# A trunk layer whose attention opens in a written-out order: keys first, two queries inside the first steps, modulation pairs behind both heads' transposes

## The chip, the cores and the metric

The kernel runs on one core of a Trainium2 chip. The metric is device time in microseconds (us), the median of three runs; a profiled execution is one further run whose trace is read here. PE is TensorE, DVE VectorE, ACT ScalarE, POOL GpSimd, SP the engine that issues most transfers.

## The reference, cut to what matters

One layer works on 128 context tokens and 512 latent tokens of width 1024. Six modulation vectors (shift, scale and gate, twice) come from the conditioning by a matrix `w_ada` of 1024 x 6144. The attention has 16 query heads in 4 groups with one key head each, of width 64. Behind it come a short convolution, gates, an output matrix and a feed-forward part.

```python
def mixer(u, p, rope_tabs, ctx_k, ctx_v):
    z = u @ p["w_in"]
    q, k, v, b_gate, c_gate, x_in, g_att, g_conv = jnp.split(z, idx, axis=-1)
    q = rms_norm(q.reshape(B, N, N_HEADS, HEAD_DIM), p["q_norm"])
    k = rms_norm(k.reshape(B, N, N_KV_HEADS, HEAD_DIM), p["k_norm"])
    ...
        q_used = apply_axial_rope(q, rope_tabs)
        keys = jnp.concatenate([ctx_k, apply_axial_rope(k, rope_tabs)], axis=1)
        vals = jnp.concatenate([ctx_v, v], axis=1)
    att = block_attention(q_used, keys, vals) @ p["w_att_out"]
    conv = (b_gate * dwconv3(c_gate * x_in, p["conv_w"])) @ p["w_conv_out"]
    merged = jax.nn.sigmoid(g_att) * att + jax.nn.sigmoid(g_conv) * conv
    return merged @ p["w_o"], k, v

def trunk_layer(h, ada, p, rope_tabs, ctx_k, ctx_v):
    sh1, sc1, g1, sh2, sc2, g2 = jnp.split(ada, N_ADA, axis=-1)
    u = rms_norm(h, p["g_pre1"]) * (1 + sc1) + sh1
    mo, k, v = mixer(u, p, rope_tabs, ctx_k, ctx_v)
    h = h + g1 * rms_norm(mo, p["g_post1"])
    ...
```

Context tokens attend to context tokens only and carry no rotary position.

## The kernel before

The 640 tokens are five tiles of 128: tile 0 is the context, tiles 1 to 4 are latent, and a sixth key tile holds the cached keys. Every matrix product is taken three times (`mm3`, L163): both operands are split into a rounded high part and the rest, and the products high-high, high-low and low-high are summed (L164 to L166). A weight block of 128 x 1024 arrives by one transfer of 512 KB into one of three `raw` buffers. Weights that belong to `w_in` or `w_att_out` are units: `cut_hi` (L585) or `split` writes the high part on ACT and the low part, `wlo`, on DVE. The modulation blocks are used as they are. PSUM gives three double banks (`ps2`, tag s2) and two single ones (`ps1`, tag s1).

**Prologue.** Norm, first modulation, and the key and value products of all tiles (`kvp`). A scheduler orders the instructions of this part by a model of their times, and its reach goes on through the opening of the attention, to L576. From L578 on (`manual_schedule`) PE, ACT and DVE keep the order of the text. POOL and SP are ordered by the scheduler everywhere.

**Opening of the attention.** `k_post` (L543) treats one key tile: it copies the values (L544), rotates the keys (`rotate`, L434, on DVE, the last addition at L446 on DVE for keys and on POOL for queries), takes squares on ACT (L450), their sums on DVE (L456) and the factor on POOL (`factors`, L453: a scaling at L457 and a power at L458), and doubles the scaled keys side by side with four ACT instructions (L556). `k_turn` (L374, its transposes by `turn` at L371) transposes a tile on PE, copies it on ACT (L378, `KH` or `KCH`) and takes its low part on DVE (L379). `q_mm` (L482) computes a query tile of the first group with 24 matmuls (`q_part`, L472, two units of four rows each), rotates it (`q_rotate`) and takes its factor. `q_turn` (L488) transposes it at L491, and writes `QH` on ACT and `QL` on DVE (L497). The loop over t runs keys two tiles ahead of queries (`K_AHEAD`), and with queries 2 and 4 goes one modulation pair each (`EARLY`).

**Steps.** For each group g of four there are nine steps: step 0 for the context, steps 1 to 8 for two halves of the queries, two pairs of heads and two tiles. `Step` (L597) computes the scores of two heads (L505), `most` their maximum on DVE (L625), `exps` the exponential on ACT (L640), `shares` the division on POOL (L650); `turned` transposes the shares of the step before on PE (L663) and copies them (L668), and `values` (L670) multiplies them with the values. In between lie, in the text's order: query tiles 0 to 2 of the next group in steps 3, 5 and 7, and 3 and 4 in steps 0 and 2; in group 3 instead three parts of a gate (`gate_part`, L695, unit 16, kept in the raw buffer `held[0]`, L525); units 10 to 17 for the next group and the gates; and the modulation pairs. A pair (`ada_use`, L535) is two blocks, 16 matmuls each at L216, into one single bank; `ada2_keep` adds the bank to `acc` on DVE. After group 3 the second gate (`gate1_part`, L788, unit 17) is computed around the last transposes, and `cut_upto(19)` (L150) cuts units 18 and 19.

**Loads.** The order of the loads behind unit 9 is a list, `ring` (L513), of modulation blocks ("a"), units ("u") and the buffer held ("g"). `ring_used(n)` says that n entries have been read and issues loads up to three entries further on. A load goes to the buffer that the pool gives out next, and SP issues it when the buffer's last reader is done.

## Time and profile before

| | before |
|---|---|
| median of 3 runs | 1165.39 us (1165.21 to 1167.93) |
| profiled execution | 1163.74 us |
| its span in the trace | 1161.9 us |
| mean granted clock of PE | 0.987 |
| instructions in the span | 19659 |
| moved by DMA | 129.58 MB |

The span is the time from the first to the last instruction of the trace; 1.84 us of the execution lie around it. The busy share of an engine is its busy time over the span; the strip of granted clocks has 40 slices of 29 us, in tenths of full speed. A timeline row has its start, its duration, the engine, the line, the operation, output and inputs, how many equal instructions follow one another, and in brackets the idle time before it with the instruction that ended it. The attention of this kernel runs from about 68 to 297 us of the span.

### The profile page before, as it was taken

The numbers are of one execution on the slowest core, as the hardware profiler recorded it, in microseconds if no ns is written. First come the engines' busy times: TensorE is split into PE (matmuls) and PEld (weight loads), VectorE is DVE, ScalarE is ACT, GpSimd is POOL, SyncE is SP. The second block draws the span as 40 slices with busy tenths as digits, with TensorE's granted clock in tenths as the row PEclk, the third lists the DMA queues.
The fourth block names the chain that finished last, engine by engine and source line by source line (L and its number), as shares of the span: only waits on it lengthen the run. The fifth ranks groups of instructions, "written<-read, shape, count | busy, mean of one in ns | idle before, by whom it ended". The sixth has DMA issues, their size and how long they took to land. (4 is left out here: it accounts for less than half of the span.)

```text
span 1161.9 us, 19659 instructions
## 1 busy us (share of the span) xinstructions
PE 1128.8 (97%) x7949; PEld 1030.3 (89%) x7949; DVE 791.1 (68%) x1267; ACT 572.0 (49%) x987; POOL 147.4 (13%) x193
## 2 busy tenths in 40 slices
PE   7997999999999999999999999999999999999997
PEld 5785788888899999999999988999999999998785
DVE  4475666655555788988745446888877788778634
ACT  4255566665433544554542246555454555545432
POOL 1034555564000000000000012000000000000001
PEclk7997999999999999999999999999999999999999
DMA  8925231322222323323232543333332333314732
GB/s 268 264 59 172 86 111 61 110 74 74 88 72 60 91 74 92 91 73 100 83 109 74 201 144 124 95 114 114 102 100 91 95 114 102 113 60 165 245 103 90
DMA packets 181400, 129.58 MB, mean 112 GB/s; under 512 B 6274, under 2 KB 163518, under 8 KB 181310
## 3 DMA queue, kind: packets, MB, share of 16 engines
q1 hardware_dynamic: 180526, 128.04, 35.8%
q8 instruction: 62, 1.02, 0.3%
q10 hardware_dynamic: 784, 0.30, 0.1%
q14 instruction: 28, 0.23, 0.1%
HBM read 116.87 MB, written 11.45 MB: 110 GB/s over the span
## 5 line engine op out<-in xcount | busy, mean ns | idle before, releaser
L844 PE MATMUL b<-ZB,whi 128*128 128x322 f32 x1024 | 229.5, 311 | 1.7 <-DVE C L855 1.7
L844 PEld LDWEIGHTS b<-ZB,whi 128*128 128x128 f32 x1024 | 173.4, 189 | 5.5 <-DVE C L855 3.9
L844 PE MATMUL b<-ZB,wlo 128*128 128x322 f32 x512 | 159.4, 311 | 0.0
L844 PE MATMUL b<-MT,whi 128*128 128x320 f32 x608 | 134.1, 308 | 0.0
L844 PEld LDWEIGHTS b<-MT,whi 128*128 128x128 f32 x608 | 101.6, 188 | 0.0
L844 PEld LDWEIGHTS b<-ZB,wlo 128*128 128x128 f32 x512 | 96.2, 188 | 0.0
L844 PE MATMUL b<-MT,wlo 128*128 128x320 f32 x304 | 93.8, 308 | 0.0
L650 POOL TENSOR_TENSOR pr<-pr,sm 128x640 f32<-128x640 f32 x64 | 79.5, 1253 | 80.6 <-DVE sm L649 74.7
L831 ACT ACTIVATE whi<-SUM 128x1024 fp32r<-128x1024 f32 x40 | 42.2, 1055 | 81.7 <-DVE SUM L1298 79.2
L1328 DVE SCALAR_TENSOR_TENSOR Y<-C,cffn,Y 128x642 f32<-128x642 f32 x88 | 77.7, 885 | 1.8 <-ACT Y L1323 0.2
L139 DVE TENSOR_TENSOR wlo<-raw,whi 128x1024 fp32r<-128x1024 f32 (+1 forms) x33 | 36.1, 1094 | 59.9 <-ACT whi L138 59.5
L640 ACT ACTIVATE pr<-s,mx,rq 128x640 f32<-128x640 f32 x64 | 56.6, 885 | 36.4 <-DVE mx L627 36.0
L844 PE MATMUL b<-UH,whi 128*128 128x320 f32 x228 | 70.5, 309 | 0.0
L844 PE MATMUL b<-UL,whi 128*128 128x320 f32 x228 | 70.4, 309 | 0.0
L625 DVE TENSOR_REDUCE mx<-s 128x1 f32<-128x640 f32 x64 | 52.5, 820 | 26.2 <-PE s L505 26.1
L844 PE MATMUL b<-UH,wlo 128*128 128x320 f32 x228 | 70.2, 308 | 0.0
L835 DVE TENSOR_TENSOR wlo<-raw,whi 128x1024 fp32r<-128x1024 f32 (+1 forms) x51 | 50.4, 1020 | 25.0 <-ACT whi L831 24.1
L164 PE MATMUL s<-whi,UH 128*128 128x256 f32 (+1 forms) x200 | 65.5, 327 | 1.9 <-ACT UH L351 1.1
L831 ACT ACTIVATE whi<-WB 128x1024 fp32r<-128x1024 f32 x38 | 40.1, 1056 | 54.9 <-DVE WB L939 54.9
L852 ACT ACTIVATE p<-b 128x322 f32<-128x322 f32 (+1 forms) x78 | 34.2, 439 | 62.1 <-PE b L844 62.1
L165 PE MATMUL s<-wlo,UH 128*128 128x256 f32 (+1 forms) x200 | 61.8, 309 | 0.0
L166 PE MATMUL s<-whi,UL 128*128 128x256 f32 (+1 forms) x200 | 59.8, 311 | 0.0
(305 smaller groups left out, 2940.3 us busy)
## 6 DMA issues: line engine op xcount, KB each, us to landing
raw<-in_w_in_dram SPq DMA_DIRECT2D x48, 512.0 KB, 3.7
RAW<-in_w_up_dram SPq DMA_DIRECT2D x40, 512.0 KB, 4.0
raw<-in_w_ada_dram SPq DMA_DIRECT2D x32, 512.0 KB, 4.0
raw<-in_w_down_dram SPq DMA_DIRECT2D x22, 512.0 KB, 4.4
araw<-in_w_ada_dram SPq DMA_DIRECT2D x16, 512.0 KB, 7.4
actd<-Y SPq DMA_DIRECT2D x18, 321.0 KB, 2.5
AFB<-actd SPq DMA_DIRECT2D x18, 321.0 KB, 5.5
raw<-in_w_conv_out_dram SPq DMA_DIRECT2D x9, 512.0 KB, 3.3
```

What stands on the lines that cost most here:

```text
L139: V.tensor_tensor(out=lo[:, :n], in0=raw, in1=hi[:, :n].bitcast(F32), op=ALU.subtract)
L164: PE.matmul(out, ah, bh, start=start, stop=False)
L165: PE.matmul(out, ah, bl, start=False, stop=False)
L166: PE.matmul(out, al, bh, start=False, stop=stop)
L625: V.tensor_reduce(out=mx, in_=self.sc[h], axis=AX.X, op=ALU.max, negate=True)
L640: S.activation(pr, self.sc[h], AF.Exp, bias=mx, scale=rs, accum_out=sm)
L650: G.tensor_tensor(out=pr, in0=pr, in1=sm.broadcast_to((128, NTOK)), op=ALU.mult)
L831: S.activation(to[0], raw, AF.Copy)
L835: V.tensor_tensor(out=lo, in0=raw, in1=hi.bitcast(F32), op=ALU.subtract)
L844: PE.matmul(out, p[:, ws], q[:, k, :], start=start and k == 0 and n == 0, stop=stop and k == 3 and n == 2, skip_group_check=True)
L852: S.activation(t, pair[j][b], AF.Copy)
L1328: V.scalar_tensor_tensor(out=y, in0=crows(j)[i][:, d:d + NACT], scalar=cffn[:, 44 * d + o:44 * d + o + 1], in1=y, op0=ALU.mult, op1=ALU.add)
```

## The change

The order of the opening is written out by hand. `manual_schedule` is entered ahead of the attention's pool, so that PE, ACT and DVE follow the text from there on. `k_post`, `rotated`, `q_mm` and `turn` are replaced by smaller functions (`k_rotate`, `k_copies`, `k_factors`, `k_double`, `k_done`, `q_first`, `q_rotate_first`, `q_factors`), which are called in one list: keys first, in the order of tiles 0, 2, 4, 1, 3, with query tiles 0 to 2 of the first group between them. Two key tiles share a double bank for their transposes. The keys' last rotary addition goes to POOL. Key tile 3 is transposed at the start of step 0, and queries 3 and 4 of the first group are computed in steps 0 and 1. First queries use single banks only. An exponential of one element is placed ahead of the keys, and a sigmoid of one element behind the last step's first transposes.

No modulation pair is in the opening any more; each group has four, in steps 2, 4, 6, 8 of group 0 and steps 1, 4, 6, 8 of the others, behind the transposes of both heads instead of between them, and its addition follows at once. The list of loads has a new order, with units 10 and 11 first. The low cuts of units 11, 13 and 15 are taken in two halves, the second in the next step. Unit 17 is cut in step 6 of group 3 instead of step 8, and `cut_upto(19)` comes ahead of most of the second gate.

```diff
@@ -36,15 +36,11 @@
 OFF = 192
 BLKS = ((0, 320), (320, 640))
 ZB = 4
-Q2 = 2
-K_AHEAD = 2
-KADD = 1
 F_LOAD = 5
 F_TAB = 6
 XB = 4
 WARM = 20
 ROWS_AT = 2
-EARLY = (2, 4)
 SEGS = ((0, NCTX), (NCTX, NTOK))
...
         KCL = kvp_.tile([128, NKV, 128], F32R, name="KCL")
         VV = kvp_.tile([128, 6, 256], F32, name="VV")
-        def turn(x, idn):
-            p = ps1()
+        def k_turn(t, kd, p):
             for h in range(4):
-                PE.transpose(p[:, h * 128:(h + 1) * 128].bitcast(x.dtype), x[:, h].rearrange("p s d -> p (s d)"), idn)
-            return p.rearrange("p (h c) -> p h c", c=128)
-        def k_turn(t, kd):
-            p = turn(kd, ident)
+                PE.transpose(p[:, h * 128:(h + 1) * 128], kd[:, h].rearrange("p s d -> p (s d)"), ident)
+        def k_done(t, p):
+            p = p.rearrange("p (h c) -> p h c", c=128)
             c0 = 0 if t in (0, 5) else t * 128
             kh, kl = (KCH, KCL) if t == 0 else (KH[:, :, c0:c0 + 128], KL[:, :, c0:c0 + 128])
...
+    fixed = ctx.enter_context(ExitStack())
+    fixed.enter_context(tc.manual_schedule(engines={mybir.EngineType.PE, mybir.EngineType.Activation, mybir.EngineType.DVE}))
...
-            (V if i == 1 and KADD else G).tensor_tensor(out=out, in0=out, in1=tm, op=ALU.add)
+            G.tensor_tensor(out=out, in0=out, in1=tm, op=ALU.add)
...
-        def q_mm(g, t):
-            pz = (ps2() if t >= Q2 else ps1())[:, 0:256]
-            q_part(pz, g, t, range(KT))
-            q_rotate(pz, g, t)
-            factors(squares(pz), rq[g][:, t, :])
...
-        ring = [("a", i) for i in range(6)] + [("u", 10), ("u", 11)] + [("a", i) for i in range(6, 14)] + [("u", 12)]
-        ring += [("a", i) for i in (14, 15)] + [("u", 13)] + [("a", i) for i in range(16, 20)] + [("u", 14)]
-        ring += [("a", i) for i in (20, 21)] + [("u", 15)] + [("a", i) for i in range(22, 26)]
-        ring += [("a", i) for i in (26, 27)] + [("u", 16), ("g", 0)] + [("a", i) for i in range(28, 32)] + [("u", 17)]
+        def ada_raws(a, b):
+            return [("a", i) for i in range(2 * a, 2 * b)]
+        ring = [("u", 10), ("u", 11)] + ada_raws(0, 4) + [("u", 12)] + ada_raws(4, 5) + [("u", 13)] + ada_raws(5, 8) + [("u", 14)]
+        ring += ada_raws(8, 9) + [("u", 15)] + ada_raws(9, 12) + ada_raws(12, 13) + [("u", 16), ("g", 0)] + ada_raws(13, 14)
+        ring += [("u", 17)] + ada_raws(14, 16)
...
-        ring_load(2)
-        kds = {}
-        def k_post(t):
-            S.activation(VV[:, 5 if t == 0 else t, :], kvp[t][:, 256:512], AF.Copy)
-            if t < 3:
+        ring_load(3)
+        warm = at.tile([128, 1], F32, name="warm", bufs=1)
+        S.activation(warm, mhalf[:, 0:1], AF.Exp)
+        kds, kfs, rks, sqs, pzs = {}, {}, {}, {}, {}
+        def k_rotate(t):
+            if t in (0, 2):
+                room = wide([128, 2, NKV, HD], "room")
+                kf, tm = room[:, 0], room[:, 1]
+                kds[t] = wide([128, NKV, 2, HD], "room")
+            else:
                 room = at.tile([128, 5, 256], F32, tag="PT", name=nm("room"), bufs=3)
                 kf, tm = (room[:, i, :].rearrange("p (h d) -> p h d", d=HD) for i in range(2))
-                kd = room[:, 2:4, :].rearrange("p a (b s d) -> p (a b) s d", s=2, d=HD)
-            else:
-                room = wide([128, 2, NKV, HD], "room")
-                kf, tm = room[:, 0], room[:, 1]
-                kd = wide([128, NKV, 2, HD], "room")
-            rk = at.tile([128, 4], F32, tag="rk", name=nm("rk"), bufs=NT)
-            rotated(kvp[t][:, 0:256], t, 1, kf, tm, rk)
+                kds[t] = room[:, 2:4, :].rearrange("p a (b s d) -> p (a b) s d", s=2, d=HD)
+            kfs[t] = kf
+            rks[t] = at.tile([128, 4], F32, tag="rk", name=nm("rk"), bufs=NT)
+            rotate(kvp[t][:, 0:256], t, 1, kf, tm)
+        def k_copies(t):
+            sqs[t] = squares(kvp[t][:, 0:256])
+            S.activation(VV[:, 5 if t == 0 else t, :], kvp[t][:, 256:512], AF.Copy)
+        def k_factors(t):
+            factors(sqs.pop(t), rks[t])
+        def k_double(t):
             for h in range(NKV):
-                S.activation(kd[:, h], kf[:, h:h + 1, :].broadcast_to((128, 2, HD)), AF.Copy, scale=rk[:, h:h + 1])
+                S.activation(kds[t][:, h], kfs[t][:, h:h + 1, :].broadcast_to((128, 2, HD)), AF.Copy, scale=rks[t][:, h:h + 1])
             if t == 0:
                 nc.scalar.dma_start(new_v.rearrange("t h d -> t (h d)"), VV[:, 5, :])
-                nc.scalar.dma_start(new_k, kd[:, :, 0, :])
-            kds[t] = kd
-        for t in range(NT + K_AHEAD):
-            if t < NT:
-                k_post(t)
-            i = t - K_AHEAD
-            if i < 0:
-                continue
-            q_mm(0, i)
-            if i in EARLY:
-                ada_use(EARLY.index(i))()
-            k_turn(i, kds[i])
-            if i > 0:
-                q_turn(0, i - 1)()
-        q_turn(0, NT - 1)()
-        fixed = ctx.enter_context(ExitStack())
-        fixed.enter_context(tc.manual_schedule(engines={mybir.EngineType.PE, mybir.EngineType.Activation, mybir.EngineType.DVE}))
+                nc.scalar.dma_start(new_k, kds[t][:, :, 0, :])
+        def q_first(t):
+            pzs[t] = ps1()[:, 0:256]
+            q_part(pzs[t], 0, t, range(KT))
+        def q_rotate_first(t):
+            q_rotate(pzs[t], 0, t)
+            sqs["q", t] = squares(pzs[t])
+        def q_factors(t):
+            factors(sqs.pop(("q", t)), rq[0][:, t, :])
+        q_first(0)
+        k_rotate(0)
+        k_copies(0)
+        k_rotate(2)
+        k_factors(0)
+        k_copies(2)
+        k_rotate(4)
+        k_factors(2)
+        k_copies(4)
+        k_rotate(1)
+        k_factors(4)
+        k_double(0)
+        k_copies(1)
+        q_first(1)
+        k_rotate(3)
+        k_factors(1)
+        k_double(2)
+        k_copies(3)
+        q_rotate_first(0)
+        k_factors(3)
+        q_factors(0)
+        p02 = ps2()
+        k_turn(0, kds[0], p02[:, 0:512])
+        k_turn(2, kds[2], p02[:, 512:1024])
+        k_double(4)
+        k_done(0, p02[:, 0:512])
+        k_done(2, p02[:, 512:1024])
+        q_first(2)
+        q_rotate_first(1)
+        q_factors(1)
+        low = q_turn(0, 0)
+        low()
+        k_double(1)
+        p41 = ps2()
+        k_turn(4, kds[4], p41[:, 0:512])
+        k_turn(1, kds[1], p41[:, 512:1024])
+        k_done(4, p41[:, 0:512])
+        k_double(3)
+        k_done(1, p41[:, 512:1024])
+        low = q_turn(0, 1)
+        low()
+        q_rotate_first(2)
+        q_factors(2)
...
-            def low():
-                V.tensor_tensor(out=lo, in0=raw, in1=hi.bitcast(F32), op=ALU.subtract)
-                ring_used(1)
+            def low(a=0, b=1024):
+                V.tensor_tensor(out=lo[:, a:b], in0=raw[:, a:b], in1=hi[:, a:b].bitcast(F32), op=ALU.subtract)
+                if b == 1024:
+                    ring_used(1)
...
-        n_ada, last, after1, after2 = len(EARLY), None, [], []
+        n_ada, last, halves = 0, None, []
+        after1, after2 = [], []
         for g in range(NKV):
             if g + 1 < NKV:
                 q_begin(g + 1)
             for i in range(9):
                 low1, low2, late_hi = [], [], []
                 st = Step(g) if i == 0 else Step(g, ((i - 1) // 4, (i - 1) // 2 % 2, (i - 1) % 2))
-                turn = {0: (g, 2) if g else None, 2: (g, 3) if g else None, 4: (g, 4) if g else None}.get(i)
-                if g + 1 < NKV and i in (5, 7):
-                    turn = (g + 1, (i - 5) // 2)
-                if turn and i != 2:
-                    low1.append(q_turn(*turn))
+                first = {0: (g, 2) if g else None, 5: (g, 4)}.get(i)
+                then = {0: None if g else (0, 2), 2: (g, 3), 5: (g + 1, 0), 7: (g + 1, 1)}.get(i)
+                if then and then[0] == NKV:
+                    then = None
+                if g == 0 and i == 0:
+                    p = ps1()
+                    k_turn(3, kds[3], p)
+                    k_done(3, p)
+                if first:
+                    low1.append(q_turn(*first))
                 if i == 2:
                     hi, lo = values(g)
                     hi()
...
                 for h in range(1 if st.ctx else 2):
                     st.most(h)
                     st.exps(h)
-                for f in low1:
+                for f in low1 + halves:
                     f()
+                halves = []
                 qt = None
                 if g + 1 < NKV and i in (3, 5, 7):
                     qt = (g + 1, (i - 3) // 2)
-                elif g and i in (0, 2):
-                    qt = (g, 3 + i // 2)
+                elif i == 0 or i == (2 if g else 1):
+                    qt = (g, 3 if i == 0 else 4)
                 blk = (i - 3) // 2 if g + 1 == NKV and i in (3, 5, 7) else None
                 if i in (4, 6, 8) or (i == 1 and g):
                     hi, lo = values(*((g - 1, 3) if i == 1 else (g, (i - 4) // 2)))
...
                     q_part(pz, *qt, range(4, KT))
                 if blk is not None:
                     gate_part(pz, c0, c1, range(4, KT))
-                if i in ((0, 2, 4, 6, 8) if g == 0 else (1, 4, 6)):
-                    low2.append(ada_use(n_ada))
-                    n_ada += 1
-                if turn and i == 2:
-                    low2.append(q_turn(*turn))
                 if not st.ctx:
                     st.shares(1)
-                u = {1: 10 + 2 * g, 2: 11 + 2 * g}.get(i) if g + 1 < NKV else {2: 16, 8: 17}.get(i)
+                u = {1: 10 + 2 * g, 2: 11 + 2 * g}.get(i) if g + 1 < NKV else {2: 16, 6: 17}.get(i)
                 if u:
-                    low2.append(cut_hi(u))
+                    low = cut_hi(u)
+                    if i == 2 and g + 1 < NKV:
+                        low2.append(lambda low=low: low(0, 512))
+                        halves = [lambda low=low: low(512, 1024)]
+                    else:
+                        low2.append(low)
+                if then and then != (0, 2):
+                    low2.append(q_turn(*then))
                 for f in low2:
                     f()
                 for f in after2:
...
                 if last and not last.ctx:
                     last.turned(1)()
                 after1, after2 = [], []
+                if i in (4, 6, 8) or i == (1 if g else 2):
+                    ada_use(n_ada)()
+                    n_ada += 1
                 if qt:
                     def rotation(pz=pz, qt=qt):
                         q_rotate(pz, *qt)
...
                         rotation()
                 if blk is not None:
                     S.activation(held[0][:, c0:c1], pz, AF.Copy)
+                if then == (0, 2):
+                    low = q_turn(0, 2)
+                    low()
                 last = st
         assert 2 * n_ada == 4 * KT and at_ring[0] == len(ring)
         state["limit"], state["next"] = 1 << 20, 18
...
         gate1_part(0, range(4))
         ada2_fold(acc)
         last.turned(0)(True)
+        S.activation(warm, mhalf[:, 0:1], AF.Sigmoid)
+        cut_upto(19)
         gate1_part(0, range(4, KT))
         last.turned(1)()
         gate1_part(1, range(4))
         hi, lo = values(NKV - 1, 3)
         hi()
         lo()
-        cut_upto(19)
         gate1_part(1, range(4, KT))
     atts.close()
```

More of the change, by code (lines that the diff above doesn't have):

```diff
@@ L417, in trunk_layer @@
             if f == F_TAB:
-                k_turn(5, ck)
+                p = ps1()
+                k_turn(5, ck, p)
+                k_done(5, p)
                 ptr = ps1()
@@ L458, in factors @@
             G.tensor_tensor(out=rstd, in0=ssq, in1=mhalf[:, :4], op=ALU.pow)
-        def rotated(pz, t, i, out, tm, rstd):
-            rotate(pz, t, i, out, tm)
-            factors(squares(pz), rstd)
         QH, QL, rq, qfs = {}, {}, {}, {}
@@ L705, in trunk_layer @@
                 st = Step(g) if i == 0 else Step(g, ((i - 1) // 4, (i - 1) // 2 % 2, (i - 1) % 2))
[L706 to L710 removed]
+                first = {0: (g, 2) if g else None, 5: (g, 4)}.get(i)
[3 more added lines that the diff above has]
+                if g == 0 and i == 0:
+                    p = ps1()
+                    k_turn(3, kds[3], p)
+                    k_done(3, p)
+                if first:
+                    low1.append(q_turn(*first))
                 if i == 2:
```

## The prediction

> **What bounds the kernel now.** I read the page first: the busy shares and the strip of granted clocks.
>
> ```profile
> PE 1128.8 (97%) x7949; PEld 1030.3 (89%) x7949; DVE 791.1 (68%) x1267; ACT 572.0 (49%) x987; POOL 147.4 (13%) x193
> PEclk7997999999999999999999999999999999999999
> ```
>
> TensorE is the bound. What can be won is its idle time, and busy time that passes at a lowered clock: the fourth slice of the strip (87 to 116 us) is such a place, and it is where the rewritten order ends. So I cut that stretch, and the attention stage behind it, into windows (the columns are busy us and instructions of PE, PEld, DVE, ACT and POOL, then the clock, the DMA share and GB/s).
>
> ```profile
> 68.00:88.00 20.00, 18.77 (x177) 17.33 (x175) 13.62 (x42) 12.95 (x39) 11.19 (x19) 1.00 0.24 66
> 88.00:92.00 4.00, 1.49 (x34) 1.01 (x34) 2.55 (x8) 3.97 (x13) 2.49 (x4) 1.00 0.46 136
> 92.00:96.00 4.00, 2.07 (x20) 1.52 (x24) 2.08 (x6) 1.57 (x5) 2.32 (x4) 0.75 0.78 247
> 96.00:100.00 4.00, 4.00 (x44) 3.07 (x32) 1.37 (x3) 0.00 (x0) 0.00 (x0) 0.50 0.60 172
> 100.00:104.00 4.00, 2.57 (x14) 1.85 (x12) 1.73 (x7) 3.31 (x6) 2.38 (x2) 0.50 0.32 96
> 104.00:108.00 4.00, 3.60 (x32) 2.24 (x29) 3.86 (x8) 2.17 (x5) 0.44 (x2) 0.54 0.39 111
> 108.00:112.00 4.00, 3.02 (x38) 2.46 (x39) 2.42 (x5) 1.82 (x4) 2.11 (x2) 1.00 0.73 213
> 112.00:297.00 185.00, 180.70 (x1870) 148.56 (x1869) 113.48 (x306) 117.24 (x252) 104.02 (x105) 1.00 0.29 85
> ```
>
> Of the 24 us from 88 to 112, PE is idle for 24 - (1.49+2.07+4.00+2.57+3.60+3.02) = 7.25 us. The clock is at half for 2 + 4 + 4 + 3.7 = 13.7 us, with about 10.9 us of busy PE in it, of which half, 5.4 us, would not be needed at full clock. From 112 to 297 the idle time is 185 - 180.7 = 4.3 us in all, so there nearly everything is PE's own work and moved work keeps its price. PE's own timeline gives the single waits (in brackets, with what ended them) and the prices of its groups:
>
> ```profile
> 80.91 0.36 PE L164 MATMUL s<-whi,UH 128*128 128x256 f32 x1
> ...
> 83.94 1.08 PE L216 MATMUL s<-raw,s 128*32 128x128 f32 x32
> ...
> 106.51 1.08 PE L216 MATMUL s<-raw,s 128*32 128x128 f32 x16
> 108.98 0.54 PE L216 MATMUL s<-raw,s 128*32 128x128 f32 x12 [1.39 <-DMA raw<-in_w_ada_dram]
> ...
> 110.25 0.41 PE L505 MATMUL s<-KH,QH 64*128 64x320 f32 x2
> ...
> 166.44 0.41 PE L505 MATMUL s<-KH,QH 64*128 64x320 f32 x1 [0.59 <-ACT PT L668]
> ...
> 294.24 0.42 PE L164 MATMUL s<-UH,whi 128*128 128x320 f32 x1 [0.80 <-ACT whi L589]
> ...
> 296.29 0.41 PE L166 MATMUL s<-UH,wlo 128*128 128x320 f32 x1 [1.50 <-DVE wlo L592]
> ```
>
> The last two are the end of the stage: unit 17 is cut in step 8, too late for gate 1, and PE stands for 2.3 us. The row at 108.98 is the pattern that matters below: a modulation pair whose block is loaded only when another buffer has just come free.
>
> **Part 1, the opening (68 to 112 us).** The same matmuls run; what differs is their order and what each waits for. A first query is 24 matmuls (80.91 to 83.94: 3.0 us). Keys are now prepared all together, and their chain runs over POOL, whose order is not written by hand. Its prices, and those of the other engines:
>
> ```profile
> L458 POOL TENSOR_TENSOR rk<-ssq,mhalf 128x4 f32<-128x4 f32 x5 | 5.1, 1012 | 0.3
> ...
> L446 POOL TENSOR_TENSOR qf<-qf,zt 128x256 f32<-128x256 f32 x4 | 2.9, 732 | 3.4 <-DVE qf L445 3.3
> L457 POOL TENSOR_SCALAR ssq<-ssq 128x4 f32<-128x4 f32 x10 | 2.0, 203 | 62.2 <-DMA raw<-in_w_ada_dram 58.1 <-DVE ssq L456 3.6
> ```
> ```profile
> 69.59 0.42 DVE L456 TENSOR_REDUCE ssq<-sq 128x4 f32<-128x256 f32 x1 [0.79 <-ACT sq L450]
> 69.92 0.48 DVE L443 TENSOR_TENSOR room<-s,tabk 128x128 f32<-128x128 f32 x2
> 70.32 0.41 DVE L445 TENSOR_TENSOR room<-s,tabk 128x256 f32<-128x256 f32 x1
> ...
> 71.71 0.41 DVE L446 TENSOR_TENSOR room<-room 128x256 f32<-128x256 f32 x1
> ```
> ```profile
> 103.72 1.45 DVE L592 TENSOR_TENSOR wlo<-raw,whi 128x1024 fp32r<-128x1024 f32 x1 [1.27 <-ACT whi L589]
> ```
> ```profile
> 73.97 1.28 ACT L556 ACTIVATE room<-room,rk 128x128 f32<-128x128 f32 x4 [0.31 <-POOL rk L458]
> ...
> 88.60 1.28 ACT L634 ACT_TABLE_LOAD   x1
> ```
>
> The four key additions go from VectorE (0.41 each, the row at 71.71) to POOL (0.73 each): 2.9 us more on POOL, ahead of the factors (0.20 + 1.01 per tile). In the changed program POOL does an addition, a factor pair (1.21), an addition, 0.20, an addition, 0.20 and the power (1.01) before tile 2's factor: 0.73+1.21+0.73+0.20+0.73+0.20+1.01 = 4.8 us. It can begin when the first rotated tile leaves VectorE: at 70.73 in before, behind a reduction that waited 0.79 for squares; the changed order puts the rotation ahead of that, so near 69.8. It ends near 74.6; ScalarE then doubles tile 2 (a quarter of 1.28 per head). PE, two queries (3.0 each) from where before has its first, is through them and tile 0's transposes near 73.8 by my estimate. So its first wait is about 1.5 us.
>
> By the same hand chain (prices above, 0.4 per copy or square, order from the program) I get eight more. The largest two: the first query's transposes wait for the bank of query 1, which is free once it is rotated and squared. Its rotation stands on VectorE behind the low parts of key tiles 0 and 2, each behind ScalarE's copy: from 78.0, 0.6 + 0.7 + 0.6 + 0.7 (half the 1.45 that a cut of 1024 columns takes in the row at 103.72), some 0.9 of rotation and 0.4 of square end at 81.9, and PE is done with query 2 at 79.8: 2.1. And the transposes of query tile 3 in step 2 wait for the bank of query 4, whose rotation stands behind the low cut of unit 10 (1.45) and the turned context shares: 2.3. The rest: query 2 for the squares of query 0, 0.7; key tile 1 for its copy, 0.4; key tile 3 for the bank that the low part of query tile 1 frees, 1.5; query 3 for squares, 0.65; query 4 in step 1 for squares behind the context exponentials, 1.5; the transposes of step 2 for the exponentials of step 1, 1.3. The exponential's table load (1.28 at 88.60) moves ahead of the keys, where ScalarE waits for PE: 0. Together 1.5 + 2.1 + 2.3 + 0.7 + 0.4 + 1.5 + 0.65 + 1.5 + 1.3 = 12 us, strewn over 73 to 107 us. So many in 34 us should again bring down the clock; I put two stretches of 3.4 us at half, 1.7 us lost in each, against four before. That makes 12 + 3.4 = 15.4 us lost. Before lost 7.25 + 5.4 in 88 to 112 and 20 - 18.77 = 1.23 in 68 to 88: 13.9. **Opening: +1.5 us.** Bounds: half my waits and one slow stretch give 6 + 1.7 - 13.9 = -6.2; all of them with four slow stretches 18.8 - 13.9 = +4.9.
>
> With two early modulation pairs, one pair of step 0 and one query's transposes gone from it, step 3 should begin its scores near 110.25 - 3.5 + 1.5 = 108 (104 to 110). That is no gain: the pairs cost 1.0 each (32 matmuls, 83.94 to 84.95) wherever they stand, and from 112 on PE has 98% of its time full. The later loop runs 4 pairs in every group instead of 5, 3, 3, 3 plus two, the same 16.
>
> **Part 2, steps of the later groups.** A pair's sum now frees its bank later: the fourth query of step 2 in groups 1 and 2 waits for that addition behind other VectorE work, about 0.9 to 1.3 by the prices above, where the scores there wait 0.59 now (the row at 166.44): +0.3 each, **+0.6**, bounds 0 and 1.4. A short wait at gate 16 in group 3 changes its cause and not its size: 0. The halved cut of units 11, 13 and 15 lets the maximum of the next step in between; VectorE is busy 113 of 185 us there: 0, bounds -0.3 and +0.3.
>
> **Part 3, one self-made wait.** In the changed order of loads the raw buffers, of which one is held from group 3 on, come out such that the 30th modulation block goes into the buffer of the 29th. Both belong to one pair, the one of step 6 of group 3, now behind both heads' transposes: its load can be issued only when PE has read the first half, and PE's next instruction is the second half. Nothing covers it. The price is a lone load, 512 KB. In before the same kind of load waits for a low cut, that of the row at 103.72. From its end at 105.17 to PE's restart at 108.98 are 3.81 us, of which only 1.39 showed there, since other matmuls lay in between. Here none do: **+3.8**. Bounds: 2.4, the 3.81 less one 1.4 that may pass in PE's last matmul and the restart, and 4.4, that much the slower from a load beside others.
>
> **Part 4, the clock after it.** Not shown alone in before: a bare gap of 3.8 us. Nearest rows are the first lowering of the run and its neighbours:
>
> ```profile
> 5.30:8.70 3.40, 1.64 (x13) 1.22 (x12) 1.51 (x2) 2.84 (x7) 1.91 (x5) 1.00 1.03 415
> 8.70:12.10 3.40, 3.38 (x16) 3.27 (x16) 2.73 (x6) 2.62 (x7) 2.82 (x6) 0.50 1.15 315
> 12.10:15.50 3.40, 3.40 (x54) 2.53 (x56) 2.74 (x7) 1.58 (x3) 0.06 (x1) 1.00 1.21 290
> ```
>
> A stretch of 3.4 us with 1.64 busy is followed by one at half, and a full one ends it: 1.7 us lost. The opening shows the dear end: four stretches, 6.8 lost. A gap of 3.8 spans one stretch or parts of two, and PE's work after it is dense (98%), so I take one stretch, 1.7, and in one case of three a second: **+2.3**, bounds 0 and 6.8.
>
> The Trainium skill has a rule here ("TensorE: Matmul & The Clock Gate", Part 1): the clock is judged in free-running windows of some 3.4 us, a wholly idle one halves it and a busy one restores it. The rows at 5.30 and 8.70 agree in the length, but there the clock fell behind a stretch that was half busy. By the page alone a gap of 3.8 us holds a whole window in 0.4 of 3.4 cases, and this term would be 0.2, the sum 2.1 lower.
>
> **Part 5, the end.** Unit 17 is cut in step 6, so 0.80 + 1.50 = **-2.3** goes; what is late next is unit 18, whose load waits for the last pair in step 8 but whose reader comes a whole gate 1 later: 0. The final cuts, made earlier, take small waits on low parts: **-0.4**, bounds -0.8 and 0.
>
> **Sum.** The profiled execution took 1163.74 us (span 1161.9 and 1.84 around it), 1.65 below the median of 1165.39. 1163.74 + 1.5 + 0.6 + 3.8 + 2.3 - 2.3 - 0.4 = **1169.2**, which is 3.8 over the median of the runs. A measurement of this kernel can tell about 0.3%, 3.5 us, from no change: slower begins at 1168.9, faster below 1161.9. The forecast stands just over the limit, with 1167 to 1172 as its own range (opening +0.5 to +3, load 3.0 to 4.4).
>
> **Rivals.** *The opening goes through* (0.14): place, 73 to 107 us; half the waits vanish because ScalarE and POOL run further ahead than my chain has them, and one stretch is slow. Price -6.2, and one slow stretch behind the load: 1163.74 - 6.2 + 0.6 + 3.8 + 1.7 - 2.7 = 1160.9. It decides if step 3's scores begin before 103. For it: 13.9 us are there to be won. Against: POOL's chain alone outlasts what PE has to do meanwhile.
>
> *The clock holds behind the load wait* (0.25): the gap lies across two stretches, both busy enough, and the strip stays at 1.00: 1169.2 - 2.3 = 1166.9, or 1165.2 with one slow stretch less in the opening too; I take 1166. For it: PE is dense on both sides of the gap. Against: the rows at 5.30 and 8.70, where a stretch busy by half was enough. The skill's page named above sides with this rival.
>
> *The clock stays down behind the load wait* (0.13): the opening's 13.7 us at half repeat, 6.8 lost in place of 2.3: 1173.7. For it: nothing but the opening's rows; against: the opening had waits all through it.
>
> *The load isn't late* (0.03): the block lands in another buffer, the change doesn't do what I read from it, and parts 3 and 4 go: 1163.1.
>
> **Numbers.** The forecast has 0.45, four fifths of it over 1168.9. Slower: 0.36 + 0.13 = 0.49. Same: its lowest fifth 0.09, the clock that holds 0.25, the load not late 0.03: 0.37. Faster: 0.14. The range from 1163 to 1173 leaves out the first rival and about half of the third, 0.2 in all.
>
> **What would show it.** In the changed profile: a wait of PE of 3.4 to 4.4 us for DMA at the modulation matmul in the last third of group 3 (near 275 to 285 us), a clock of 0.5 behind it; no wait for `wlo` at gate 1; step 3's scores at 104 to 110; fewer slow stretches between 84 and 112; key doubling as the first releaser of PE near 75. I am wrong if the scores of step 3 start after 111, if no DMA wait is seen in group 3, or if the clock there stays 1.00 and the time still grows.

## The result, and the profile after

The changed kernel takes 1170.15 us (median of 9 runs, 1167.21 to 1171.18), the kernel before in the same comparison 1166.09 (9 runs, 1164.19 to 1167.93). The ratio is 1.0033, 95% interval 1.0022 to 1.0043: slower by 3.9 us. Forecast were 1169.2, or 3.8 over the median of before.

The profiled execution took 1170.93 us, span 1169.1. Against the profile of before that is 7.2 us more, but 1163.74 lies below before's nine runs, so the two profiles show the places and the medians the size.

Page of the changed kernel, busy shares and granted clock:

```profile
PE 1131.1 (97%) x7949; PEld 1034.7 (89%) x7949; DVE 791.9 (68%) x1266; ACT 573.0 (49%) x989; POOL 150.3 (13%) x197
PEclk8997999999899999999999999999999999999999
```

The work of PE is the same to 2.3 us. Windows of the changed kernel (columns as in the prediction):

```profile
68.00:88.00 20.00, 15.45 (x101) 12.98 (x99) 9.63 (x28) 12.41 (x38) 11.96 (x19) 0.91 0.14 39
88.00:112.00 24.00, 19.37 (x146) 16.23 (x146) 15.35 (x37) 11.55 (x28) 11.36 (x14) 0.72 0.14 40
112.00:284.00 172.00, 168.68 (x1822) 141.16 (x1824) 108.68 (x294) 110.94 (x239) 98.48 (x101) 1.00 0.34 100
284.00:288.10 4.10, 0.45 (x20) 0.18 (x13) 2.51 (x4) 1.24 (x2) 1.28 (x2) 1.00 0.48 142
288.10:304.00 15.90, 15.90 (x137) 13.23 (x137) 5.75 (x15) 6.52 (x14) 4.22 (x4) 0.68 0.22 63
```

In the opening the idle time has moved forward: 4.55 us in 68 to 88 (1.23 before) and 4.63 in 88 to 112 (7.25 before), 9.2 in all against 8.5. Then comes one hole, 284 to 288.1, and behind it 15.9 us without a gap at a mean clock of 0.68. The waits of the opening and the hole on PE's timeline (the row of SP is the load's issue, from SP's own timeline):

```profile
76.72 1.21 PE L367 MATMUL s<-ident,room 128*128 128x128 f32 x4 [1.96 <-ACT room L561]
78.40 0.58 PE L160 MATMUL s<-whi,UH 128*128 128x256 f32 x1 [0.48 <-ACT sq L450]
...
83.32 0.44 PE L481 MATMUL s<-ident,qf 128*128 128x128 f32 x2 [0.55 <-ACT sq L450]
...
84.52 1.20 PE L367 MATMUL s<-ident,room 128*128 128x128 f32 x4 [0.33 <-ACT room L561]
...
89.11 1.12 PE L367 MATMUL s<-ident,room 128*128 128x128 f32 x4 [2.35 <-DVE QL L487]
...
105.10 0.67 PE L481 MATMUL s<-ident,qf 128*128 128x128 f32 x2 [2.00 <-ACT sq L450]
107.03 1.30 PE L707 MATMUL s<-ident,pr 128*128 128x128 f32 x5 [1.25 <-issue]
...
110.12 0.63 PE L495 MATMUL s<-KH,QH 64*128 64x320 f32 x2
...
283.77 0.64 PE L212 MATMUL s<-raw,s 128*32 128x128 f32 x16
...
284.48 0.37 SPq L206 DMA_DIRECT2D raw<-in_w_ada_dram  x1
...
288.07 0.64 PE L212 MATMUL s<-raw,s 128*32 128x128 f32 x16 [3.65 <-DMA raw<-in_w_ada_dram]
...
302.96 1.08 PE L212 MATMUL s<-raw,s 128*32 128x128 f32 x32
```

Line numbers are four lower in the first third of the changed file and differ behind it: L160 is a product of `mm3`, L367 a key's transposes, L481 a query's, L495 the scores, L561 the doubling, L707 the shares' transposes, L212 the modulation. Of the nine waits of the opening that the prediction names, seven are there; query 3 (at 90.31) doesn't wait and query 4 (at 96.94) waits 0.18 us, where 0.65 and 1.5 were forecast. The largest of all is the load wait of 3.65 us, in the step and from the cause that the prediction gave: PE has read the first half of the pair at 284.41, the load for the second half is issued at 284.48, and PE goes on at 288.07. Step 3's scores start at 110.12, where before has 110.25 with three pairs and a query's transposes more behind it. The last wait of before, gate 1 for unit 17, is gone: no idle time behind 288.1.

### The profile page after: what moved, and what is told of

Same layout as the page of the kernel before. It is cut to its first block, busy times and chain, and to the rows that moved or that the text cites. A ratio compares the mean times of both kernels' runs of the same rounds, so it can differ in the third digit from the quotient of the medians.

```text
span 1169.1 us, 19638 instructions
## 1 busy us (share of the span) xinstructions
PE 1131.1 (97%) x7949; PEld 1034.7 (89%) x7949; DVE 791.9 (68%) x1266; ACT 573.0 (49%) x989; POOL 150.3 (13%) x197
## 5 line engine op out<-in xcount | busy, mean ns | idle before, releaser
L160 PE MATMUL s<-whi,UH 128*128 128x256 f32 (+1 forms) x200 | 67.4, 337 | 6.1 <-ACT UH L347 2.5
```

The costliest lines, as they stand in the source:

```text
L160: PE.matmul(out, ah, bh, start=start, stop=False)
```

## The experiments

Every run below was timed against the kernel before on its own chip, so the ratios are what is compared; the changed kernel stands at 1.0033.

**Unit 17 one step earlier (u17_step5).** The 30th block then waits for the low cut of unit 17 in step 5, not for PE in step 6.

```diff
-                u = {1: 10 + 2 * g, 2: 11 + 2 * g}.get(i) if g + 1 < NKV else {2: 16, 6: 17}.get(i)
+                u = {1: 10 + 2 * g, 2: 11 + 2 * g}.get(i) if g + 1 < NKV else {2: 16, 5: 17}.get(i)
```

> The changed kernel with unit 17 cut in step 5 of group 3 instead of step 6, so that the 30th modulation block is loaded a step earlier. Theory (the self-made load wait and the lowered clock behind it cost 3.65 us and some 4.5 us): both go, 1170.2 - 8 = 1162 (ratio to before 0.9965), no wait for DMA in group 3, clock 1.00 from 112 us to the end of the stage. Rival (the loss comes from the opening and the moved pairs, the clock behind the wait costs next to nothing): 1170.2 - 3.7 = 1166.5, ratio 1.000.

Measured: 1160.56 us, ratio 0.9958 (0.9943 to 0.9973); repeated below, 0.9963. The timeline and a window of this kernel:

```profile
283.14 0.65 PE L212 MATMUL s<-raw,s 128*32 128x128 f32 x16
283.94 0.64 PE L212 MATMUL s<-raw,s 128*32 128x128 f32 x16 [0.16 <-DMA raw<-in_w_ada_dram]
...
294.13 1.08 PE L212 MATMUL s<-raw,s 128*32 128x128 f32 x32
```
```profile
283.00:304.00 21.00, 20.84 (x222) 17.59 (x222) 9.85 (x28) 10.63 (x21) 7.04 (x6) 1.00 0.44 129
```

The wait is 0.16 us and the clock 1.00 from 283 to 304 us. The mean of the two ratios, 0.9960, is 0.0073 below the changed kernel: 8.5 us for the one load. The wait became 3.5 us shorter (3.65 less 0.16), which leaves 5.0 to the clock. The traces say nearly the same without the ratios: from the pair of step 6 to that of step 8 PE takes 19.19 us in the changed kernel (283.77 to 302.96) and 10.99 here, 8.2 less, of which 4.7 is no wait. One number in the order turns a kernel that is slower than before into one that is faster.

**The wide block of the gate behind the wait (wide_gate_last).** The load wait stays; what PE does behind it changes from matmuls of 128 columns to matmuls of 256.

```diff
-                blk = (i - 3) // 2 if g + 1 == NKV and i in (3, 5, 7) else None
+                blk = (7 - i) // 2 if g + 1 == NKV and i in (3, 5, 7) else None
```

> The changed kernel with the three blocks of gate 16 in the other order: the one of 128 columns in step 3, one of 256 columns in step 7, right behind the load wait. Theory (the clock stayed at half for three stretches because the matmuls of 128 columns that follow the wait keep the array too thinly filled for the clock to return): one stretch at half instead of three, the load wait still 3.65, 1170.2 - 3.4 = 1166.8 (0.8 to 1.0 of 3.4 us won). Rival (the clock needs that time whatever follows, or the transposes of shares are what hold it down): three stretches again, 1170.

Measured: 1166.83, ratio 1.0009 (0.9997 to 1.0020), 0.0024 or 2.8 us below the changed kernel. Stretches of 3.41 us around the wait, first in the changed kernel, then with the wide block last:

```profile
286.07:289.48 3.41, 1.41 (x26) 1.22 (x28) 0.86 (x2) 0.00 (x0) 0.00 (x0) 1.00 0.89 264
289.48:292.89 3.41, 3.41 (x20) 3.07 (x17) 2.04 (x5) 1.78 (x4) 0.53 (x1) 0.50 0.60 173
292.89:296.31 3.42, 3.42 (x19) 3.42 (x18) 0.16 (x1) 0.83 (x3) 1.94 (x2) 0.50 0.03 5
296.31:299.72 3.41, 3.41 (x21) 2.56 (x21) 0.46 (x1) 0.87 (x2) 0.00 (x0) 0.50 0.00 0
299.72:303.10 3.38, 3.38 (x36) 2.30 (x35) 2.16 (x6) 2.18 (x5) 1.25 (x1) 1.00 0.00 0
```
```profile
283.65:287.06 3.41, 1.35 (x26) 1.16 (x28) 0.71 (x2) 0.00 (x0) 0.00 (x0) 1.00 0.85 249
287.06:290.47 3.41, 3.41 (x19) 3.08 (x16) 2.05 (x5) 1.67 (x3) 0.42 (x1) 0.50 0.59 172
290.47:293.88 3.41, 3.41 (x35) 3.23 (x33) 0.16 (x1) 1.73 (x5) 2.05 (x2) 1.00 0.02 5
```

Three slow stretches become one. In both kernels the first is busy to the last digit; what differs is the size of the matmuls, which take turns every 0.21 us whether they have 128 columns (changed kernel, first fence) or 256 (second):

```profile
290.15 0.41 PE L161 MATMUL s<-UL,whi 128*128 128x128 f32 x1
290.36 0.41 PE L162 MATMUL s<-UH,wlo 128*128 128x128 f32 x1
```
```profile
287.94 0.41 PE L161 MATMUL s<-UL,whi 128*128 128x256 f32 x1
288.15 0.41 PE L162 MATMUL s<-UH,wlo 128*128 128x256 f32 x1
```

At half clock a matmul of 128 columns takes as long as one of 256, so half as many columns pass in the same busy time. That this order of the blocks decides is shown by the exchange; what exactly the chip counts is not. The other runs agree with the two profiles: where the clock is either full or half, as in these windows, a run's mean granted clock gives its time at half as (1 - clock) x 2 x time, which is 37.2 us on average in the nine runs of the changed kernel and 30.7 in the twelve of this one, 6.5 less against 6.8 (two stretches) in the profiles. The Trainium skill ("TensorE: Matmul & The Clock Gate", Part 1) calls the warm-up a matter of some 3.4 us of time and not of the number of matmuls; two stretches here were busy throughout and the clock stayed at 0.50 behind each, so busy time alone doesn't bring it back.

**Before with unit 17 in step 7 (before_u17_step7).**

```diff
-                u = {1: 10 + 2 * g, 2: 11 + 2 * g}.get(i) if g + 1 < NKV else {2: 16, 8: 17}.get(i)
+                u = {1: 10 + 2 * g, 2: 11 + 2 * g}.get(i) if g + 1 < NKV else {2: 16, 7: 17}.get(i)
```

> The kernel before with unit 17 cut in step 7 instead of step 8 and nothing else. Theory (the last term of the sum): the waits of gate 1 for its cut, 0.80 + 1.50 us, go, 1166.1 - 2.3 = 1163.8, ratio 0.998. Rival (ScalarE and VectorE hold the cut up in step 7 and delay the exponentials, or something else is late at gate 1): 1166 or more.

Measured: 1162.51, ratio 0.9975 (0.9962 to 0.9988), 2.9 us; the end's term of 2.3 lies in the interval. In the waits of PE from 112 to 304 us (total, times, longest), first before, then this kernel, both lines of gate 1 shrink to the 0.6 that gate 16 has in group 3:

```profile
PE s L166 <- DVE wlo L592: 2.1, 2, 1.5
...
PE s L164 <- ACT whi L589: 0.8, 1, 0.8
```
```profile
PE s L166 <- DVE wlo L592: 0.6, 1, 0.6
```

**The pairs' old place (pairs_between).**

```diff
+                if i in (4, 6, 8) or i == (1 if g else 2):
+                    low2.append(ada_use(n_ada))
+                    n_ada += 1
                 if not st.ctx:
                     st.shares(1)
...
-                if i in (4, 6, 8) or i == (1 if g else 2):
-                    ada_use(n_ada)()
-                    n_ada += 1
```

> As u17_step5, but with the modulation pairs at their old place between the transposes of the two heads. It tells what the place of the pairs is worth, in steps that are the same otherwise. Theory (PE is full, a pair costs 1.0 wherever it stands, and only the wait for the pair's sum in step 2 of groups 1 and 2 changes, about 0.6 in all): within 1 us of u17_step5, rather below it. Rival (the place matters: between the transposes the pair covers POOL's division for the second head): 2 to 4 us above u17_step5.

Measured: 1163.36, ratio 0.9985 (0.9974 to 0.9995), 0.0025 or 2.9 us above u17_step5: the rival's size. Its reason isn't the one: a pair that covers the division would save a wait in this version, and the waits from 112 us on, u17_step5 (its second run) first, add up to the same 3.5 and 3.4 us:

```profile
PE s L160 <- DVE acc L233: 1.1, 1, 1.1
PE s L160 <- DVE acc L231: 1.1, 1, 1.1
PE s L160 <- DVE QL L487: 1.1, 3, 0.5
PE s L212 <- DMA raw<-in_w_ada_dram: 0.2, 1, 0.2
```
```profile
PE s L160 <- DVE QL L487: 2.7, 3, 1.1
PE s L212 <- DMA raw<-in_w_ada_dram: 0.7, 1, 0.7
```

The two waits for the sum (`acc`) are the 1.1 us each that the prediction put at 0.9 to 1.3; they go, and the wait for query 3's low part takes their place. What grows is PE's own work. From the first scores of step 4 to gate 1, u17_step5_b first, the same 1931 matmuls keep PE busy 1.8 us longer:

```profile
113.78:293.57 179.79, 176.27 (x1931) 146.43 (x1930) 113.42 (x304) 116.03 (x249) 102.34 (x104) 1.00 0.34 101
```
```profile
113.04:294.47 181.43, 178.06 (x1931) 146.54 (x1931) 112.64 (x305) 115.28 (x247) 102.15 (x104) 1.00 0.34 100
```

One pair shows how. Behind both heads the ten transposes run as one row and the pair follows, 2.26 us from 128.43 to the next scores at 130.69. Between the heads the row is broken: five transposes at 127.84, the pair, five more at 129.55, 2.41 us to the scores at 130.25.

```profile
128.43 1.31 PE L707 MATMUL s<-ident,pr 128*128 128x128 f32 x10
129.68 1.08 PE L212 MATMUL s<-raw,s 128*32 128x128 f32 x32
```
```profile
127.84 0.77 PE L707 MATMUL s<-ident,pr 128*128 128x128 f32 x5
```

So 1.6 of the 2.9 us (181.43 less 179.79) lie here. The mean clocks give 25.8 us at half against 22.8 for u17_step5, worth up to 1.5 more; that the place caused this isn't shown. Next stands the place alone in the kernel before.

**The pairs' new place in the kernel before (before_pairs_behind).** The edit is the reverse of the one above, on before_u17_step7, in the steps that before has.

> before_u17_step7 with one edit: the modulation pairs stand behind the transposes of both heads, as in the changed kernel, in the steps where the kernel before has them. Theory (the place itself is worth what pairs_between lost, 2 to 3 us): 0.9950 of before. Rival (the place only helped the changed opening, where the pair stood between query 4's squares and step 2's transposes, and the clock there): the same as before_u17_step7, 0.9975, or worse by the wait of query 4 for the pair's sum, 1.1 us in each of groups 1 and 2.

Measured: 1162.44, ratio 0.9977 (0.9968 to 0.9986), the same as before_u17_step7. In total the place is worth nothing there, as the prediction had it, but by two effects that cancel. From step 4 to gate 1, before_u17_step7 first:

```profile
117.97:296.37 178.40, 176.30 (x1833) 144.93 (x1833) 109.99 (x297) 113.86 (x246) 100.53 (x103) 1.00 0.29 87
```
```profile
116.66:295.37 178.71, 174.39 (x1834) 144.84 (x1833) 110.94 (x298) 114.22 (x247) 101.15 (x104) 1.00 0.30 89
```

PE is busy 1.9 us less and idle 2.2 us more; the new waits are those for the pair's sum, 2.5 us in all. In the changed kernel the same place saves the same work, and there the waits for the sum replace others of the same size.

**Low cuts in one piece (cut_whole).**

```diff
-                    if i == 2 and g + 1 < NKV:
+                    if False:
                         low2.append(lambda low=low: low(0, 512))
                         halves = [lambda low=low: low(512, 1024)]
```

> As u17_step5, with the low cuts of units 11, 13 and 15 in one piece again. Theory (VectorE has room there): within 1 us of u17_step5, 0.996. Rival (the half cut lets the next maximum in early, and PE waits for exponentials without it): 0.5 us more per group, 0.9975.

Measured: 1162.79, ratio 0.9982 (0.9972 to 0.9992), 2.6 us above u17_step5: the rival. The waits from 112 us on show where half of it is; to be read against the row `QL` of u17_step5 above, 1.1:

```profile
PE s L160 <- DVE QL L487: 2.5, 3, 0.8
```

The prediction had 0 for the halves. They save 1.4 us of waits for a query's low part, which stands behind the cut on VectorE. For the other half the trace shows no row; the mean clocks give 26.4 us at half here and 23.4 in u17_step5's two comparisons, worth up to 1.5.

**The opening (u17_step5_b, keyadd_vector, banks_early, banks_early_rot4, all_four).** Each edit stands on u17_step5, which was run again beside the next three.

> The kernel with unit 17 in step 5 once more, on the chip of the next three, which build on it. All theories: 0.996 of before.

Measured: 1161.35, ratio 0.9963 (0.9950 to 0.9975). PE's clock in its profile is 1.00 while query 2 runs, and the wait at the first query's transposes is then 1.81 us where the changed kernel's profile has 0.55:

```profile
82.30 0.44 PE L481 MATMUL s<-ident,qf 128*128 128x128 f32 x2 [1.81 <-ACT sq L450]
```

A slow stretch ahead of a wait swallows it: PE comes later by what it would have waited. The window of the opening (two stretches at half here, five in the changed kernel's profile) has 44 - 32.85 = 11.15 us of idle time, against 9.2 there:

```profile
68.00:112.00 44.00, 32.85 (x263) 28.03 (x262) 27.00 (x70) 24.98 (x68) 23.75 (x33) 0.92 0.18 50
```

```diff
-            G.tensor_tensor(out=out, in0=out, in1=tm, op=ALU.add)
+            (V if i == 1 else G).tensor_tensor(out=out, in0=out, in1=tm, op=ALU.add)
```

> As u17_step5, with the keys' last rotary addition on VectorE again (0.41 each) instead of POOL (0.74 each, four of them, three ahead of the factor of tile 2). Theory (POOL's chain sets the first wait of the opening, 1.96 us for the doubled tile 2): POOL's factor for tile 2 is ready some 2 us sooner, that wait falls below 0.5, and 1 to 1.5 us are won if PE isn't held by the next wait. Rival (the next wait takes it up, since the squares of query 1 and the bank of key tile 3 come later anyway): within 0.5 us of u17_step5.

Measured: 1160.35, ratio 0.9952 (0.9939 to 0.9964), 0.0011 below its neighbour, within the intervals, so theory and rival can't be told apart by the time. The wait for the doubled tile 2 falls from 1.96 to 1.25, not below 0.5 as the theory had it:

```profile
73.93 1.20 PE L367 MATMUL s<-ident,room 128*128 128x128 f32 x4 [1.25 <-ACT room L561]
```

```diff
         k_double(4)
+        q_rotate_first(1)
         k_done(0, p02[:, 0:512])
         k_done(2, p02[:, 512:1024])
         q_first(2)
-        q_rotate_first(1)
...
                 if g == 0 and i == 0:
-                    p = ps1()
+                    p = ps2()[:, 0:512]
```

> As u17_step5, with key tile 3 transposed into a double bank (not the single one that the low part of query tile 1 frees) and query 1 rotated and squared ahead of the copies of key tiles 0 and 2. It takes away the largest wait of the opening, 2.35 us of key tile 3, and the 0.5 of the first query's transposes. Theory (the strewn waits keep the clock down in the opening, so a wait removed gives its own length and part of a slow stretch): 2.5 to 4 us below u17_step5. Rival (the chain over VectorE and ScalarE is what is long, and PE waits for it one place further on): within 1 us.

Measured: 1160.22, ratio 0.9945 (0.9932 to 0.9958), 0.0018 or 2.1 us below its neighbour. That lies between the theory's 2.5 to 4 and the rival's 1. The waits of the first query's transposes (1.81) and of key tile 3 (2.35) are gone, and half of the latter comes back one place further on, at query 3:

```profile
89.25 0.39 PE L160 MATMUL s<-whi,UH 128*128 128x256 f32 x1 [1.21 <-DVE QL L487]
```

```diff
+                sq4 = None
+                if qt == (0, 4):
+                    q_rotate(pz, *qt)
+                    sq4 = squares(pz)
                 for f in low2:
                     f()
...
-                if qt:
+                if sq4 is not None:
+                    after2.append(lambda sq=sq4: factors(sq, rq[0][:, 4, :]))
+                elif qt:
```

> As banks_early, and query 4 of the first group is rotated and squared ahead of the low cut of unit 10 in step 1, so that the transposes of query tile 3 in step 2 find their bank free (2.0 us now). Theory: that wait goes, 1 to 2 us below banks_early. Rival (the low cut comes 0.9 later, with it the load of the second modulation block, and PE waits for that block in step 2, or for the transposes of step 1): the same as banks_early or above.

Measured: 1158.40, ratio 0.9935 (0.9923 to 0.9947), 0.0010 below banks_early. The intervals of the two overlap. The wait of 2.0 us in step 2 is gone; the transposes of step 1's shares behind it then wait 2.62 in place of 1.49, and the load of the second block does not show. The row names POOL, but POOL's factor had ended at 102.39. PE goes on 0.1 us behind the end of step 2's first exponential on ScalarE (102.76 here, 105.86 in banks_early with PE at 105.96), and that exponential waited for its maximum, which stands on VectorE behind the low cut of unit 10:

```profile
102.86 0.74 PE L707 MATMUL s<-ident,pr 128*128 128x128 f32 x5 [2.62 <-POOL rq L458]
```

all_four is banks_early_rot4 with the edit of keyadd_vector, to see whether the gains add up.

> The changed kernel with all that helped: unit 17 in step 5, key tile 3 in a double bank and query 1 squared early, query 4 rotated early, the keys' addition on VectorE. Theory (waits of the opening add up, since PE is what bounds it): 0.9935 less another 0.0005 to 0.001, near 0.993. Rival (with the later waits removed POOL's chain is hidden, or the addition of 0.4 each now delays VectorE): the same as banks_early_rot4, 0.9935.

Measured: 1158.39, ratio 0.9942 (0.9929 to 0.9955): not told apart from banks_early_rot4, and not the 0.993 of the theory. These two are the fastest versions, some 7 us below before.

## Why the prediction was right, and where two of its terms were not

The total was right, 3.8 over the median against 3.9. Each term of the sum has its run:

| term | forecast | measured | from |
|---|---|---|---|
| opening, later steps, final cuts | +1.7 | -1.8 | u17_step5 (0.9960) less before_u17_step7 (0.9975) |
| load wait | +3.8 | +3.5 | the row at 288.07, less the 0.16 left in u17_step5 |
| clock behind it | +2.3 | +5.0 | 1.0033 less 0.9960 is 8.5, less 3.5; the traces say 4.7 |
| end | -2.3 | -2.9 | before_u17_step7 |

The measured column adds up to the total by the way it is made. The ratios' intervals make each difference uncertain by some 2 us, so the load wait and the end agree. The first and the third term were off by 3.5 and 2.7 us in opposite directions and cancelled: that the forecast came within 0.1 us is luck.

*The load wait* (part 3): place, cause and size as forecast, and shown by taking it away.

*The clock behind it* (part 4): the mechanism was right and the term too small. "I take one stretch, 1.7, and in one case of three a second" failed, because dense work was taken to bring the clock back after one stretch. There were three slow stretches, 10.24 us; the first two were filled mostly by matmuls of 128 columns, and wide_gate_last shows the one stretch of the forecast where the matmuls are wide. The rival by which the clock holds is refuted in this profile, and the dear rival (6.8) lay nearer to the measured 4.7 to 5.0 than the forecast did.

Where the first term went wrong can be read from four marks on PE's timeline, us from the start of the span:

| | last high-high product of 512 columns | first scores of step 3 | gate 1 | end |
|---|---|---|---|---|
| before | 67.99 | 110.25 | 294.24 | 1161.9 |
| before_u17_step7 | 69.13 | 112.22 | 296.37 | 1162.3 |
| changed | 68.91 | 110.12 | 303.97 | 1169.1 |
| u17_step5 | 67.75 | 109.24 | 295.14 | 1160.4 |
| u17_step5_b | 67.86 | 107.86 | 293.57 | 1158.8 |

*The opening* (part 1), between the first two marks: 42.3 and 43.1 us before, 41.2, 41.5 and 40.0 in the changed order, on average 1.8 less. The forecast was 2.0 less, 3.5 of work moved out and 1.5 lost. So the net was right as far as these profiles can tell, but not its two parts. The changed kernel's profile has 9.2 us of idle time, not 12, and five stretches at half clock (from 77.86, 88.09, 91.50, 105.16 and 108.57), 17.1 us, not two; before has four, 13.7 us. The second profile of the same opening, u17_step5_b, has the two stretches of the forecast and 11.15 us of idle time, near the 12, with query 3's wait at 0.55 (0.65 forecast). The list of waits was nearly right, then, for an opening with two slow stretches, and every further one swallows part of it. How many there are differs between executions of one program: u17_step5's two profiles have five and two. POOL's chain was right to half a microsecond: the power of tile 2's factor ends 5.3 us after the first addition begins, 4.8 forecast, and the wait behind it is 1.96, 1.5 forecast.

```profile
70.94 0.73 POOL L446 TENSOR_TENSOR room<-room 128x256 f32<-128x256 f32 x1 [58.63 <-DMA raw<-in_w_ada_dram]
...
75.20 1.02 POOL L458 TENSOR_TENSOR rk<-ssq,mhalf 128x4 f32<-128x4 f32 x1
```

*Later steps* (parts 1 and 2), from step 3 to gate 1: 184.2 us in before_u17_step7, 185.9 and 185.7 in u17_step5's two profiles, 1.7 more where 3.5 of moved work and 0.6 of waits were forecast. The step that failed is that a pair costs 1.0 "wherever they stand" and that moved work keeps its price. The waits grew by 1.7 us in all (1.8 to 3.5; the wait for the sum came as forecast, 1.1 us twice), but PE's work did not grow: from step 4 to gate 1 it is busy 176.27 us with 1931 matmuls, and in before_u17_step7 176.30 with 1833. The place behind both heads' transposes gives 1.8 of these 3.5 us, as pairs_between shows; where the rest comes from is not traced. The halved cuts were put at 0 and save 1.4 us of waits.

*The end* (part 5): shown; unit 18 caused no wait, as forecast. Behind gate 1 the final cuts took 0.7 us (866.0 to 865.3 and 865.2), 0.4 forecast.

The marks add up to about 0.8 us less than before_u17_step7, the ratios to 1.8; the difference lies within what the ratios can tell. By the mean clocks u17_step5 has 22.8 and 24.0 us at half in its two comparisons and before_u17_step7 28.9, worth up to half of the difference of 5.5; in which part of the run the clocks don't say.

The other rivals: the load that isn't late fails on the wait of 3.65 us. The opening that goes through fails on its own sign: step 3's scores start at 110.12, not before 103. Without the load wait the changed kernel would have stood at 0.9960, faster by 4.7 us and near the 1160.9 of that rival (0.14), but it is the load wait that is gone there, and the opening's waits are still there. Two of the signs named were missed narrowly: the scores were to start by 110, and the wait near 275 to 285 ends at 288. A third, fewer slow stretches between 84 and 112, isn't there in this profile, which has four as before has.

## What to carry to other kernels

When an order of loads is rewritten, write down for each load which instruction frees its buffer and which one needs it; if both belong to the same piece of work on the bounding engine, the whole transfer is a hole, however much is prefetched elsewhere. Price the hole with the clock that follows it, and look at what runs behind it: wide matmuls bring the clock back in one stretch, narrow ones may not. A list of waits and a number of slow stretches don't add up: an engine at half clock comes later to the next wait and waits less. And work moved on a full engine keeps its price only if it interrupts nothing: here the same pairs cost less behind a row of transposes than inside it.

## What the runs showed of the hardware

A stretch of 3.41 us that is 0.41 busy (1.41 of 3.41, the row at 286.07) is followed by one at half clock, and two stretches busy throughout, mostly with matmuls of 128 columns, leave it there (289.48 and 292.89). The third, with scores of 320 columns, is the last. The busy share alone doesn't decide when the clock falls: stretches with 1.76 us busy (changed kernel, from 282.66) and 1.61 (wide_gate_last, from 280.24) were followed by full clock, stretches with 1.64 (before, from 5.30) and 2.08 (changed kernel, from 84.68) by half.

A gap of 3.65 us cost 8.5 us by the ratios and 8.2 by the traces with narrow work behind it. With wide work behind it the loss over u17_step5 was 5.7 us (1.0009 less 0.9960) by the ratios and 5.4 by the traces (16.40 less 10.99 between the same two pairs), 3.7 of it the wait itself.
